# RWKV state kept block-diagonal, with neighbouring chunks of odd channel tiles in each other's place

## The chip, the core and the metric

The kernel runs on one core of a Trainium2 chip. The metric is device time in microseconds (us) of one execution, as the median of several runs. Engines are named as the profile names them: PE is TensorE's matmul (PEld its weight load), DVE is VectorE, ACT is ScalarE, POOL is GpSimd and SP is SyncE, which here only issues DMAs. L788 is line 788 of the kernel before.

## What is computed

One decoder layer over 1024 tokens and 1024 channels: a norm, one wide projection, RWKV-7 time mixing beside an attention that selects 256 keys by an indexer, gates that merge the two, an output projection, and a SwiGLU feed-forward part between two norms. The change is in the time mixing. It has 8 heads of 64 channels, and each head carries a state of 64 by 64 from token to token:

```python
def step(state, inp):
    r_t, d_t, k_t, v_t, kk_t, a_t = inp
    sa = jnp.einsum('bhij,bhj->bhi', state, -kk_t)
    state = (state * d_t[:, :, None, :]
             + sa[..., None] * (kk_t * a_t)[:, :, None, :]
             + v_t[..., None] * k_t[:, :, None, :])
    y_t = jnp.einsum('bhij,bhj->bhi', state, r_t)
    return state, y_t

_, y = lax.scan(step, state0, (tm(r_h), tm(decay), tm(k_h), tm(v_h), tm(kk), tm(a_h)))
```

Then y is normalised per head, a bonus term is added, and the sum is multiplied by a gate.

## The kernel before, in words

**Layout.** Everything is kept transposed, with channels on partitions. A channel tile has 128 channels, so it holds two heads; the four tiles 0 to 3 of the time mixing hold the eight heads, and a tile with an odd number is called an odd tile here. The big matmuls take two fp32r parts of each operand, high and low (`mm3`, L135): columns of 512 tokens, three products for each of the eight contraction tiles.

**The order of PE** is the program's own, written by hand. The big matmuls are generators that stand in a list named `fill`; `pump(n)` (L163) takes some n matmuls from it, and the recurrence calls it between its dependent products. The other engines' orders are made by the scheduler from the order of the program.

**Projections.** `proj_rwkv` (L302) makes the fourteen tiles r, k, v (four each), the low-rank inputs of decay and a (one tile) and the gate (one tile). Each result is shifted by a token into a staging tile `stg` (two buffers) and stored to DRAM (`d_rw`) by one DMA of 512 KB on SP's queue (L307; for decay and a at L404).

**The time mixing** (`rwkv`, L517) goes through the 1024 tokens in four quarters of 256, and each quarter has four chunks of 64 tokens. Two neighbouring chunks are a pair. A quarter loads its tiles back (L528), makes tanh of the low-rank products (L551), sums the log decay by chunk (L558), takes exponentials (P, L562), copies the decay over a whole chunk to PC (L566), and builds for every chunk two tables on the token axis, read rows and key rows (`AR`, `BK`), the masked products between them (`MT`, L667), a transposed copy (`NAT`, L686), and the inverse of a triangular matrix for each head and chunk (`TT`, L698 to L759).

Which half of 128 rows a chunk uses goes by its parity `pa` in the pair: `ba = 64 - 64 * pa` are the rows of the solve, `kb = 64 * pa` those of keys and outputs. All heads of a step have the same `ba`.

**The recurrence** (L778 to L845) has one step for each chunk, sixteen in all:

1. *read*: `AR` times the state, 8 products (64 rows contracted, 128 results, 64 columns), even and odd heads into two PSUM tiles (L787 to L790);
2. DVE adds the `ba` half to `rhs` (L794), ACT copies the `kb` half to the output buffer `y2` (L795); then a pump of 6 or 8;
3. *solve*: `TT` times `rhs`, 8 products of 64 by 64 (L800), which ACT copies, negated, into `UV` (L802); then a pump, or the `finish` of the pair before;
4. *update*: `NAT` times `UV`, 8 products (128 rows contracted, 64 results, 64 columns) (L810); DVE adds the old state (L813) and multiplies by PC (L814), into one of two state buffers; then a pump of 7 or 9 after the first chunk of a pair.

After both chunks of a pair come the *output* `MT` times `UV` (L821), `inner` (L741: the next pair's `rhs`, 16 products of 64 by 64 at L745, for both chunks in turn), the norm of y (L828 to L839), and later `finish` (L762): a transpose back, scale and bias by ACT (L771), the bonus by DVE (L773), the gate (L774), and a store to DRAM that the merge of that half reads.

The state's tile is `[128, 4, 64]`: for tile ct, rows 0 to 63 hold the even head's state and rows 64 to 127 the odd head's.

Of the kernel before, what the change touches and what calls it, by code (L numbers as in the profile page):

```python
# [11 lines left out]
F32 = mybir.dt.float32  # L12
# [6 lines left out]
AF = mybir.ActivationFunctionType  # L19
ALU = mybir.AluOpType  # L20
# [3 lines left out]
S = 1024  # L24
# [25 lines left out]
def block_kernel(ctx: ExitStack, tc: tile.TileContext, ins: dict, outT: bass.AP, stop=None, dbg=None):  # L50
# [15 lines left out]
    kc = cp.tile([128, 2, 128], F32, name="kc")  # L66
    state = cp.tile([128, 4, 64], F32, tag="S", name="S", bufs=2)
    G.dma_start(kc, ins["consts"][:, 0:2, :])
# [221 lines left out]
    def shifted(st, half, ct, x):  # L290
# [8 lines left out]
        else:  # L299
            V.scalar_tensor_tensor(s[:, 0:1], halo[:, ct:ct + 1], mu, s[:, 0:1], op0=ALU.mult, op1=ALU.add)  # L300

    def proj_rwkv(us, pj, groups):  # L302
        for g0, n in groups:
            for j in range(n):
                st = stage(pj)
                yield from proj(g0 + j, us, lambda half, ps: shifted(st, half, g0 + j, ps))
                SY.dma_start(d_rw[g0][j], st.rearrange("p h t -> p (h t)"))  # L307

# [183 lines left out]
    V.memset(state, 0.0)  # L492
    sref = [state]

# [22 lines left out]
    def rwkv(half, p, consts, ready=None):  # L517
# [5 lines left out]
        for q in range(2 * half, 2 * half + 2):  # L523
# [17 lines left out]
            for c in range(2):  # L541
                pss = [mix(), mix()]
                for e in range(2):
                    ct = 2 * c + e
                    for i, ps in enumerate(pss):
                        half_ = slice(64 * i, 64 * i + 64)
                        T.matmul(ps[:, e * 256:(e + 1) * 256], wup[half_, ct * 128:(ct + 1) * 128], wa[half_, :],
                                 start=True, stop=True)
                for i, t in enumerate((L, ta)):
                    for ct in (2 * c, 2 * c + 1):  # L550
                        A.activation(t[:, ct, :], pss[i][:, ct % 2 * 256:ct % 2 * 256 + 256], AF.Tanh, scale=0.5,  # L551
                                     bias=hb[:, 4 * i + ct:4 * i + ct + 1])
            sg = gd
# [126 lines left out]
            NAT = []  # L680
# [81 lines left out]
            def finish(pr, yc, y2):  # L762
# [7 lines left out]
                for ct in range(4):  # L770
                    A.activation(yT[:, ct, :], pt[:, ct * 128:(ct + 1) * 128], AF.Identity,  # L771
                                 scale=par[:, P_LG + ct:P_LG + ct + 1], bias=par[:, P_LB + ct:P_LB + ct + 1])
                V.tensor_tensor(yT, yT, bon[:, :, pr * 128:(pr + 1) * 128], op=ALU.add)  # L773
                V.tensor_tensor(yT, yT, pg.rearrange("p (c t) -> p c t", c=4), op=ALU.mult)  # L774
# [4 lines left out]
            for pr in range(2):  # L779
                yb = p.tile([128, 2, 512], F32, tag=("P", "x6")[pr], name="yb")  # L780
                yc, y2 = yb[:, 0, :], yb[:, 1, :]
                for pa in range(2):
                    c = 2 * pr + pa
                    ba, kb = 64 - 64 * pa, 64 * pa
                    st = sref[0]
                    as_ = [mix(), mix()]
                    for h, ct, ro, hc in hd:  # L787
                        T.matmul(as_[h % 2][:, ct * 64:ct * 64 + 64],  # L788
                                 AR[ro, ct, c, :, :].rearrange("p s t -> p (s t)"), st[ro, ct, :],
                                 start=True, stop=True)  # L790
                    for g in range(2):
                        a4 = as_[g][:, 0:256].rearrange("p (c t) -> p c t", c=4)
                        r4 = rhs.rearrange("p (c g t) -> p c g t", c=4, g=2)[ba:ba + 64, :, g, :]
                        V.tensor_tensor(r4, a4[ba:ba + 64], r4, op=ALU.add)  # L794
                        A.activation(y2.rearrange("p (c g t) -> p c g t", c=4, g=2)[kb:kb + 64, :, g, :],  # L795
                                     a4[kb:kb + 64], AF.Copy)
                    pump(6 if half == 0 else 8)
                    ps = mix()
                    for h, ct, ro, hc in hd:
                        T.matmul(ps[ba:ba + 64, hc], TT[ba:ba + 64, pr, h, :], rhs[ba:ba + 64, hc],  # L800
                                 start=True, stop=True)
                    A.activation(UV[pr][ba:ba + 64, pa, :], ps[ba:ba + 64, :], AF.Copy, scale=-1.0)  # L802
                    if late and pa == 1:
# [5 lines left out]
                    for h, ct, ro, hc in hd:  # L809
                        T.matmul(ps[ro, ct * 64:ct * 64 + 64], NAT[pr][:, pa, hc], UV[pr][:, pa, hc],  # L810
                                 start=True, stop=True)
                    new = cp.tile([128, 4, 64], F32, tag="S", name="S", bufs=2)
                    V.tensor_tensor(new, ps[:, 0:256].rearrange("p (c t) -> p c t", c=4), st, op=ALU.add)  # L813
                    V.tensor_tensor(new, new, PC[:, :, c:c + 1].to_broadcast([128, 4, 64]), op=ALU.mult)  # L814
                    sref[0] = new
                    if pa == 0:
# [675 lines left out]
```

## Time and profile before

| What | Value |
|---|---|
| Median of 3 runs | 1748.55 us (1747.58 to 1753.21) |
| The profiled execution's own time | 1748.71 us |
| Its span in the profile | 1746.9 us |
| Busy: PE, DVE, ACT | 98%, 64%, 48% of the span |
| Recurrence, first product to last | 446.9 to about 951 us, in four stretches |
| Matmul records of the solve, read, update | 256 each (two for each f32 product) |
| Clock granted to TensorE | 0.996 of full speed |

The profile shows one execution. Its rows give an engine, a line, an operation, what it writes and reads (`out<-in`), a count, and times; a group's row has busy us, mean ns, and the idle time before it with what ended that. Matmuls are pipelined, so their durations overlap; the distance from one start to the next says what a block costs.

### The profile page before, as it was taken

The numbers are of one execution on the slowest core, as the hardware profiler recorded it, in microseconds if no ns is written. First come the engines' busy times: TensorE is split into PE (matmuls) and PEld (weight loads), VectorE is DVE, ScalarE is ACT, GpSimd is POOL, SyncE is SP. The second block draws the span as 40 slices with busy tenths as digits, with TensorE's granted clock in tenths as the row PEclk, the third lists the DMA queues.
The fourth block names the chain that finished last, engine by engine and source line by source line (L and its number), as shares of the span: only waits on it lengthen the run. The fifth ranks groups of instructions, "written<-read, shape, count | busy, mean of one in ns | idle before, by whom it ended". The sixth has DMA issues, their size and how long they took to land.

```text
span 1746.9 us, 26692 instructions
## 1 busy us (share of the span) xinstructions
PE 1708.1 (98%) x10156; PEld 1410.3 (81%) x10156; DVE 1114.3 (64%) x2133; ACT 833.3 (48%) x1547; POOL 100.5 (6%) x123
## 2 busy tenths in 40 slices
PE   8999999999999998999999999999999999999997
PEld 6888888778878776878787888888788888888887
DVE  6789899857468567857876655445465564454464
ACT  6365998453445687645333455433234322232241
POOL 0000000010021111000100321000000000000000
PEclk9999999999999999999999999999999999999999
DMA  5542224536357535644343765173464344434442
GB/s 210 173 138 94 97 97 145 163 97 171 100 178 201 149 121 157 197 146 118 97 127 93 234 165 138 61 225 113 165 213 140 109 136 151 136 96 150 139 124 93
DMA packets 132383, 247.14 MB, mean 141 GB/s; under 512 B 36848, under 2 KB 60080, under 8 KB 132128
## 3 DMA queue, kind: packets, MB, share of 16 engines
q1 hardware_dynamic: 108896, 171.61, 31.7%
q10 hardware_dynamic: 15552, 47.75, 8.7%
q0 software_dynamic: 7808, 26.09, 5.6%
q8 instruction: 80, 1.31, 0.3%
q14 instruction: 47, 0.39, 0.1%
HBM read 192.40 MB, written 53.00 MB: 140 GB/s over the span
## 4 chain that ended last, share of the span: by engine, by line
PE 50%; issue 1%; DVE 1%; ACT 0%; POOLq 0%; POOL 0%; DVEq 0%; ACTq 0%
PE acc L145 14%; PE acc L140 13%; PE acc L141 13%; PE acc L156 3%; PE mix L1053 1%; PE mix L1029 1%; PE mix L1043 1%; PE acc L1197 0%; PE mix L800 0%; PE mix L788 0%; PE acc L1201 0%; ACT whi L114 0%; DVE h L1272 0%; PE mix L254 0%; PE mix L810 0%
## 5 line engine op out<-in xcount | busy, mean ns | idle before, releaser
L115 DVE TENSOR_TENSOR wlo<-wst,whi 128x1024 fp32r<-128x1024 f32 (+1 forms) x229 | 277.5, 1214 | 276.0 <-PE acc L145 132.7
L114 ACT ACTIVATE whi<-wst 128x1024 fp32r<-128x1024 f32 (+1 forms) x229 | 238.3, 1043 | 262.7 <-PE acc L141 186.9
L140 PE MATMUL acc<-zhi,whi 128*128 128x512 f32 x672 | 264.8, 394 | 0.0
L141 PE MATMUL acc<-zlo,whi 128*128 128x512 f32 x672 | 262.0, 390 | 0.0
L145 PE MATMUL acc<-zhi,wlo 128*128 128x512 f32 x672 | 170.2, 392 | 0.0
L140 PEld LDWEIGHTS acc<-zhi,whi 128*128 128x128 f32 x672 | 126.2, 188 | 26.8 <-issue 1.9
L141 PEld LDWEIGHTS acc<-zlo,whi 128*128 128x128 f32 x672 | 126.3, 188 | 24.8
L145 PEld LDWEIGHTS acc<-zhi,wlo 128*128 128x128 f32 x672 | 124.8, 188 | 25.4 <-issue 0.7
L140 PE MATMUL acc<-u1hi,whi 128*128 128x512 f32 x352 | 140.5, 399 | 0.1
L141 PE MATMUL acc<-u1lo,whi 128*128 128x512 f32 x352 | 137.6, 391 | 0.0
L140 PE MATMUL acc<-u0hi,whi 128*128 128x512 f32 (+1 forms) x352 | 135.5, 387 | 1.7 <-DVE tmp L323 1.7
L141 PE MATMUL acc<-u0lo,whi 128*128 128x512 f32 (+1 forms) x352 | 133.8, 383 | 0.0
L140 PE MATMUL acc<-fhi,whi 128*128 128x512 f32 (+1 forms) x318 | 114.3, 368 | 2.3 <-ACT whi L114 1.5
L141 PE MATMUL acc<-flo,whi 128*128 128x512 f32 (+1 forms) x318 | 112.9, 364 | 0.2 <-DVE flo L115 0.2
L145 PE MATMUL acc<-u1hi,wlo 128*128 128x512 f32 x352 | 90.0, 394 | 0.0
L145 PE MATMUL acc<-u0hi,wlo 128*128 128x512 f32 (+1 forms) x352 | 85.7, 384 | 0.0
L114 ACT ACTIVATE fhi<-tmp 128x512 fp32r<-128x512 f32 x44 | 27.7, 630 | 112.6 <-DVE tmp L1229 112.3
L140 PEld LDWEIGHTS acc<-u0hi,whi 128*128 128x128 f32 x352 | 66.2, 188 | 14.9 <-ACT stg L114 2.1
L140 PEld LDWEIGHTS acc<-u1hi,whi 128*128 128x128 f32 x352 | 66.2, 188 | 14.8 <-issue 1.3
L141 PEld LDWEIGHTS acc<-u1lo,whi 128*128 128x128 f32 x352 | 66.2, 188 | 12.6
L141 PEld LDWEIGHTS acc<-u0lo,whi 128*128 128x128 f32 x352 | 66.2, 188 | 12.1
L145 PEld LDWEIGHTS acc<-u1hi,wlo 128*128 128x128 f32 x352 | 64.9, 188 | 13.7 <-issue 0.9
(328 smaller groups left out, 3204.2 us busy)
## 6 DMA issues: line engine op xcount, KB each, us to landing
wst<-in_w_ffn_in SPq DMA_DIRECT2D x72, 512.0 KB, 3.6
wst<-in_w_in ACTq DMA_DIRECT2D x36, 512.0 KB, 4.5
wst<-in_w_in SPq DMA_DIRECT2D x27, 512.0 KB, 4.0
wst<-in_w_fo SPq DMA_DIRECT2D x25, 512.0 KB, 3.8
k<-d_k POOLq DMA_DIRECT2D x24, 512.0 KB, 7.9
h<-in_xT SPq DMA_DIRECT2D x32, 256.0 KB, 5.2
d_g<-tmp ACTq DMA_DIRECT2D x32, 256.0 KB, 3.4
tmp<-d_g SPq DMA_DIRECT2D x32, 256.0 KB, 3.7
```

The source lines that it names most:

```text
L114: A.activation(hi, x, AF.Copy)
L115: V.tensor_tensor(lo, x, hi.bitcast(F32), op=ALU.subtract)
L140: T.matmul(ps, whi[:, wk + k, :], ahi[:, ak + k, tok], start=k == 0, stop=False)
L141: T.matmul(ps, whi[:, wk + k, :], alo[:, ak + k, tok], start=False, stop=False)
L145: T.matmul(ps, wlo[:, wk + k, :], ahi[:, ak + k, tok], start=False, stop=k == nk - 1)
L156: T.matmul(ps, w[:, k, :], a[:, k, tok], start=k == 0 and w is whi and a is ahi, stop=k == nk - 1 and a is alo)
L1029: T.matmul(ps[:, :w], q[bi // 2][:, e, bi % 2 * 128:bi % 2 * 128 + 128], k[:, i, e, c:c + w], start=i == 0, stop=i == 1)
L1043: T.transpose(ps[:, j * 128:(j + 1) * 128], L[:, (c + j) * 128:(c + j + 1) * 128], ident)
L1053: T.matmul(py[64 * e:64 * e + 64, bi * 128:(bi + 1) * 128], v[:, j, 64 * e:64 * e + 64], pts[e][j // 4][:, j % 4, :], start=j == b, stop=j ...
```

## The change

**Storage.** For odd tiles of r, k and v the two chunks of each pair are stored in each other's place. `proj_rwkv` does this at the store, with two DMAs whose runs are 64 elements long; even tiles are stored as before. The tanh for decay and a of odd tiles writes its two halves swapped (two ACT operations of 128 columns in place of one of 256), PC is copied so that it stays in true order, and `finish` swaps back (two ACT operations for an odd tile, and the bonus in three DVE adds in place of one).

**Step.** A step still handles one true chunk of all heads. For odd tiles that chunk lies in the other slot, so its `ba` and `kb` are the other halves: `at[0]` is for even tiles, `at[1]` for odd ones. The eight heads of the solve are issued in the order 0, 2, 1, 3, 4, 6, 5, 7.

**State.** The tile becomes `[128, 4, 2, 64]`, a 128 by 128 block for each channel tile with the two heads' states on its diagonal and zeros beside them, in one buffer. The read becomes four products (128 rows contracted, 128 results, 128 columns) into one PSUM tile. The decay is multiplied into the whole state after the read; after the update's product DVE multiplies the product by PC into a `tmp` buffer and adds it to the two diagonal blocks. The core of the diff:

```diff
-    state = cp.tile([128, 4, 64], F32, tag="S", name="S", bufs=2)
+    state = cp.tile([128, 4, 2, 64], F32, name="S")
...
+    def swapped(x):
+        return x.rearrange("p (n s t) -> p n s t", s=2, t=64)
...
-                SY.dma_start(d_rw[g0][j], st.rearrange("p h t -> p (h t)"))
+                if g0 in (CT_R, CT_K, CT_V) and j % 2:
+                    d, t = (swapped(x) for x in (d_rw[g0][j], st.rearrange("p h t -> p (h t)")))
+                    for i in range(2):
+                        SY.dma_start(d[:, :, i, :], t[:, :, 1 - i, :])
+                else:
+                    SY.dma_start(d_rw[g0][j], st.rearrange("p h t -> p (h t)"))
...
-                        A.activation(t[:, ct, :], pss[i][:, ct % 2 * 256:ct % 2 * 256 + 256], AF.Tanh, scale=0.5,
-                                     bias=hb[:, 4 * i + ct:4 * i + ct + 1])
+                        x, y = pss[i][:, ct % 2 * 256:ct % 2 * 256 + 256], t[:, ct, :]
+                        xy = [(x, y)] if ct % 2 == 0 else [(swapped(x)[:, :, j, :], swapped(y)[:, :, 1 - j, :])
+                                                           for j in range(2)]
+                        for x, y in xy:
+                            A.activation(y, x, AF.Tanh, scale=0.5, bias=hb[:, 4 * i + ct:4 * i + ct + 1])
...
-            V.tensor_copy(PC, P[:, :, :, 64])
+            V.tensor_copy(PC[:, 0::2, :], P[:, 0::2, :, 64])
+            for i in range(2):
+                V.tensor_copy(PC[:, 1::2, i::2], P[:, 1::2, 1 - i::2, 64])
...
-                    A.activation(yT[:, ct, :], pt[:, ct * 128:(ct + 1) * 128], AF.Identity,
-                                 scale=par[:, P_LG + ct:P_LG + ct + 1], bias=par[:, P_LB + ct:P_LB + ct + 1])
-                V.tensor_tensor(yT, yT, bon[:, :, pr * 128:(pr + 1) * 128], op=ALU.add)
+                    x, y = pt[:, ct * 128:(ct + 1) * 128], yT[:, ct, :]
+                    xy = [(x, y)] if ct % 2 == 0 else [(x[:, 64 - 64 * i:128 - 64 * i], y[:, 64 * i:64 * i + 64])
+                                                       for i in range(2)]
+                    for x, y in xy:
+                        A.activation(y, x, AF.Identity, scale=par[:, P_LG + ct:P_LG + ct + 1],
+                                     bias=par[:, P_LB + ct:P_LB + ct + 1])
+                b = bon[:, :, pr * 128:(pr + 1) * 128]
+                V.tensor_tensor(yT[:, 0::2, :], yT[:, 0::2, :], b[:, 0::2, :], op=ALU.add)
+                for i in range(2):
+                    y = yT[:, 1::2, 64 * i:64 * i + 64]
+                    V.tensor_tensor(y, y, b[:, 1::2, 64 - 64 * i:128 - 64 * i], op=ALU.add)
...
-                    ba, kb = 64 - 64 * pa, 64 * pa
-                    st = sref[0]
-                    as_ = [mix(), mix()]
-                    for h, ct, ro, hc in hd:
-                        T.matmul(as_[h % 2][:, ct * 64:ct * 64 + 64],
-                                 AR[ro, ct, c, :, :].rearrange("p s t -> p (s t)"), st[ro, ct, :],
-                                 start=True, stop=True)
+                    at = [(pa ^ x, 64 - 64 * (pa ^ x), 64 * (pa ^ x)) for x in range(2)]
+                    as_ = mix()
+                    for ct in range(4):
+                        T.matmul(as_[:, ct * 128:(ct + 1) * 128],
+                                 AR[:, ct, 2 * pr + at[ct % 2][0], :, :].rearrange("p s t -> p (s t)"),
+                                 state[:, ct, :, :].rearrange("p e t -> p (e t)"), start=True, stop=True)
...
+                    for x, (pp, ba, kb) in enumerate(at):
+                        r4 = tiles(x, rhs[ba:ba + 64, :])
+                        V.tensor_tensor(r4, tiles(x, as_[ba:ba + 64, :]), r4, op=ALU.add)
+                    for x, (pp, ba, kb) in enumerate(at):
+                        A.activation(tiles(x, y2[kb:kb + 64, :]), tiles(x, as_[kb:kb + 64, :]), AF.Copy)
+                    V.tensor_tensor(state.rearrange("p c e t -> p c (e t)"), state.rearrange("p c e t -> p c (e t)"),
+                                    PC[:, :, c:c + 1].to_broadcast([128, 4, 128]), op=ALU.mult)
...
-                    for h, ct, ro, hc in hd:
+                    for h, ct, ro, hc in (hd[i] for i in (0, 2, 1, 3, 4, 6, 5, 7)):
+                        ba = at[ct % 2][1]
                         T.matmul(ps[ba:ba + 64, hc], TT[ba:ba + 64, pr, h, :], rhs[ba:ba + 64, hc],
                                  start=True, stop=True)
-                    A.activation(UV[pr][ba:ba + 64, pa, :], ps[ba:ba + 64, :], AF.Copy, scale=-1.0)
+                    for x, (pp, ba, kb) in enumerate(at):
+                        A.activation(tiles(x, UV[pr][ba:ba + 64, pp, :]), tiles(x, ps[ba:ba + 64, :]), AF.Copy, scale=-1.0)
...
-                    new = cp.tile([128, 4, 64], F32, tag="S", name="S", bufs=2)
-                    V.tensor_tensor(new, ps[:, 0:256].rearrange("p (c t) -> p c t", c=4), st, op=ALU.add)
-                    V.tensor_tensor(new, new, PC[:, :, c:c + 1].to_broadcast([128, 4, 64]), op=ALU.mult)
-                    sref[0] = new
+                    new = tmp()[:, 0:256].rearrange("p (c t) -> p c t", c=4)
+                    V.tensor_tensor(new, ps[:, 0:256].rearrange("p (c t) -> p c t", c=4),
+                                    PC[:, :, c:c + 1].to_broadcast([128, 4, 64]), op=ALU.mult)
+                    for e in range(2):
+                        eo = slice(64 * e, 64 * e + 64)
+                        V.tensor_tensor(state[eo, :, e, :], state[eo, :, e, :], new[eo], op=ALU.add)
```

`tiles(x, y)` takes the even (x = 0) or odd (x = 1) channel tiles' 128 columns of y. The update's product reads `NAT` and `UV` at the slot `at[ct % 2][0]`.

More of the change, by code (lines that the diff above doesn't have):

```diff
@@ L492, in block_kernel @@
     V.memset(state, 0.0)
-    sref = [state]
     def rwkv_consts(p):
@@ new lines, in rwkv, with tiles @@
+                    as_ = mix()
[3 more added lines that the diff above has]
+                                 state[:, ct, :, :].rearrange("p e t -> p (e t)"), start=True, stop=True)
+                    def tiles(x, y):
+                        return y.rearrange("p (c t) -> p c t", c=4)[:, x::2, :]
+                    for x, (pp, ba, kb) in enumerate(at):
+                        r4 = tiles(x, rhs[ba:ba + 64, :])
+                        V.tensor_tensor(r4, tiles(x, as_[ba:ba + 64, :]), r4, op=ALU.add)
@@ L809, in rwkv @@
                     for h, ct, ro, hc in hd:
-                        T.matmul(ps[ro, ct * 64:ct * 64 + 64], NAT[pr][:, pa, hc], UV[pr][:, pa, hc],
+                        pp = at[ct % 2][0]
+                        T.matmul(ps[ro, ct * 64:ct * 64 + 64], NAT[pr][:, pp, hc], UV[pr][:, pp, hc],
                                  start=True, stop=True)
-                    new = cp.tile([128, 4, 64], F32, tag="S", name="S", bufs=2)
-                    V.tensor_tensor(new, ps[:, 0:256].rearrange("p (c t) -> p c t", c=4), st, op=ALU.add)
-                    V.tensor_tensor(new, new, PC[:, :, c:c + 1].to_broadcast([128, 4, 64]), op=ALU.mult)
-                    sref[0] = new
+                    new = tmp()[:, 0:256].rearrange("p (c t) -> p c t", c=4)
[4 more added lines that the diff above has]
+                        V.tensor_tensor(state[eo, :, e, :], state[eo, :, e, :], new[eo], op=ALU.add)
                     if pa == 0:
```

6 lines of the change are left out of this document (removed).

## The prediction

> **What bounds the kernel now.** I read the page first: the engines' busy shares, the slices, the chain that ended last.
>
> ```profile
> span 1746.9 us, 26692 instructions
> PE 1708.1 (98%) x10156; PEld 1410.3 (81%) x10156; DVE 1114.3 (64%) x2133; ACT 833.3 (48%) x1547; POOL 100.5 (6%) x123
> PE   8999999999999998999999999999999999999997
> PEclk9999999999999999999999999999999999999999
> PE 50%; issue 1%; DVE 1%; ACT 0%; POOLq 0%; POOL 0%; DVEq 0%; ACTq 0%
> ```
>
> TensorE (PE) is busy in nearly every slice at nearly the full clock, and the chain runs over PE; "issue" and VectorE (DVE) have 1% each. So time taken out of PE's instruction stream should shorten the span, unless PE then stands waiting. The change is made in the recurrence, so I read next the four stretches that hold its sixteen steps. A row has the stretch and its length, then the busy us (and instructions) of PE, PE's weight load, DVE, ACT and POOL, PE's clock, the DMA share and GB/s.
>
> ```profile
> 440.00:480.00 40.00, 39.73 (x543) 32.06 (x542) 17.91 (x34) 18.60 (x38) 1.64 (x1) 1.00 0.28 92
> 590.00:640.00 50.00, 49.34 (x638) 39.56 (x636) 29.08 (x65) 42.72 (x105) 5.71 (x6) 1.00 0.29 98
> 750.00:800.00 50.00, 49.32 (x583) 39.67 (x582) 28.02 (x51) 26.84 (x50) 2.79 (x2) 1.00 0.40 118
> 915.00:960.00 45.00, 44.54 (x471) 35.92 (x464) 26.30 (x44) 16.45 (x31) 1.64 (x1) 1.00 0.30 89
> ```
>
> In all four PE is full, while DVE works 45 to 58% of the time. The small dependent products of the recurrence are spaced by fill: matmuls of 512 columns that the pump lets in. A busy PE is not PE at its peak, so I price blocks by the distance between starts in the timeline of PE, where ends, which are modelled, don't enter.
>
> ```profile
> 449.48 0.39 PE L140 MATMUL acc<-u0hi,whi 128*128 128x512 f32 x1
> 449.71 0.39 PE L141 MATMUL acc<-u0lo,whi 128*128 128x512 f32 x1
> 450.03 1.14 PE L800 MATMUL mix<-rhs,TT 64*64 64x64 f32 x16
> 451.10 0.50 PE L140 MATMUL acc<-u0hi,whi 128*128 128x512 f32 x1
> ...
> 460.17 0.69 PE L810 MATMUL mix<-UV,NAT 128*64 128x64 f32 x16
> 460.69 1.10 PE L821 MATMUL mix<-UV,MT 128*64 128x64 f32 x32
> 461.72 1.15 PE L745 MATMUL mix<-UV,MT 64*64 64x64 f32 x32
> 462.80 1.11 PE L788 MATMUL mix<-S,AR 64*128 64x64 f32 x16
> 463.84 0.50 PE L140 MATMUL acc<-u0hi,whi 128*128 128x512 f32 x1
> 464.17 0.39 PE L141 MATMUL acc<-u0lo,whi 128*128 128x512 f32 x1
> ```
>
> Here each f32 product is two records (x16 for eight heads). A fill matmul takes 449.71 - 449.48 = 0.23 us. The solve (L800) takes 451.10 - 450.03 = 1.07 us, 67 ns a record; its eight products of 64 by 64 all sit in the same quarter of the array. The block L745 has products of the same size whose rows and columns change sides from one to the next: 462.80 - 461.72 = 1.08 us for 32 records, 34 ns each. The state's read (L788) takes 463.84 - 462.80 = 1.04 us; the first fill after it takes 464.17 - 463.84 = 0.33 us, and the last one before a small block 450.03 - 449.71 = 0.32 us: about 0.1 more than 0.23 on either side, where the tile shape changes.
>
> **The change part by part.** *The solve.* With the chunks swapped in odd tiles, L800's heads go in an order that alternates the two diagonal quarters. I price it like L745, at half of 1.08, 0.54 us. Per step 1.07 - 0.54 = 0.53 us goes; sixteen steps: **8.5 us**. The bounds: nothing (records still go one after another), and 8.5.
>
> [...]
>
> *The state's read.* Four products with all 128 rows and 128 columns take the place of eight with 64 rows and 64 columns. The same shape, f32, eight records, is found where the norm's factors are spread over columns.
>
> ```profile
> 50.83 0.84 PE L145 MATMUL acc<-u1hi,wlo 128*128 128x512 f32 x3
> 51.51 1.05 PE L254 MATMUL mix<-kc,rsk 128*128 128x128 f32 x8
> 52.32 0.48 PE L140 MATMUL acc<-u0hi,whi 128*128 128x512 f32 x1
> 52.63 0.39 PE L141 MATMUL acc<-u0lo,whi 128*128 128x512 f32 x1
> ```
>
> The block takes 52.32 - 51.51 = 0.81 us, the next fill 0.31, 0.08 more than 0.23; before it three fills take 0.68, so nothing is lost on entry. That makes 0.89 us, against 0.09 + 1.04 + 0.10 = 1.23 for the read of before. Per step 0.34, sixteen steps: **5.4 us**; the bounds are 0.15 a step (2.4 us, if the entries and exits stay) and 0.34.
>
> The update (L810) and the output (L821) keep their counts and shapes: no change on PE. Nothing is added to PE. What comes next is what the step adds on DVE and ScalarE (ACT). The rows are groups of instructions between 440 and 960 us.
>
> ```profile
> L794 DVE TENSOR_TENSOR rhs<-mix,rhs 64x256 f32<-64x256 f32 x32 | 12.2, 417 | 23.4 <-PE mix L788 14.3 <-ACT TT L759 8.9
> L800 PEld LDWEIGHTS mix<-rhs,TT 64*64 64x64 f32 x256 | 16.1, 135 | 5.7 <-issue 2.5 <-DVE rhs L794 1.4 <-ACT TT L759 0.4
> L771 ACT ACTIVATE yb<-mix,par 128x128 f32<-128x128 f32 x28 | 10.7, 456 | 5.6 <-PE mix L767 5.5
> L795 ACT ACTIVATE yb<-mix 64x256 f32<-64x256 f32 x32 | 10.7, 372 | 7.1 <-DVE rhs L794 7.0
> L802 ACT ACTIVATE UV<-mix 64x512 f32<-64x512 f32 x16 | 9.5, 593 | 11.6 <-PE mix L800 10.4 <-DVE wlo L115 1.2
> L551 ACT ACTIVATE x<-mix,hb 128x256 f32<-128x256 f32 x24 | 9.2, 487 | 0.5 <-PE mix L547 0.5
> L814 DVE TENSOR_TENSOR S<-S,PC 128x256 f32<-128x256 f32 x16 | 6.8, 424 | 0.5
> L828 DVE TENSOR_TENSOR yb<-mix,yb 128x512 f32<-128x512 f32 x8 | 5.5, 686 | 0.3 <-PE mix L821 0.2
> ```
>
> - *Decaying the state* is now a multiply of 128x512 ahead of the update, 0.69 us by L828. It lies beside the solve; behind it in DVE's queue stand the weights' low parts (L115) and the adds of the fill.
> - *After the update's product* come three dependent DVE operations (a multiply of 128x256, two adds of 64x256 at 0.42 by L794) where there were two. The timeline shows the tightest place:
>
> ```profile
> 601.39 0.69 PE L810 MATMUL mix<-UV,NAT 128*64 128x64 f32 x16
> ...
> 602.13 0.42 DVE L813 TENSOR_TENSOR S<-mix,S 128x256 f32<-128x256 f32 x1 [1.21 <-PE mix L810]
> ...
> 603.16 1.11 PE L788 MATMUL mix<-S,AR 64*128 64x64 f32 x16
> ```
>
> DVE begins 0.74 us after the product's start. Three operations of 0.42 (L813, L814 and L794 agree) with their gaps are some 1.3, and some 0.1 passes until PE starts: 2.2 us, where PE comes back after 1.77. This step waits 0.4. Where PE comes back 2.63 us later (460.17 to 462.80) the third operation is covered.
> - *Read to solve.* The two adds into rhs (L794) keep their size. But PE arrives earlier: with four fills between, after 0.81 + 0.08 + 4 x 0.23 + 0.09 = 1.90 us, while the adds end at 1.05 (the read's modelled end) + 0.1 + 0.84 = 1.99. In the eight steps of half 0, which have the smaller pump, I take 0.1 each: 0.8.
> - *ACT* copies the solve's result in two halves of 64x256, 2 x 0.37 against 0.59, and the two copies of L795 now share a bank with both adds (they waited 7.0 us for DVE before, too). The cover is the four to eight fills ahead of the update, 0.9 us or more; without it 0.15 x 16 = 2.4 us.
> - *DVE's queue.* A step adds 0.69 + 0.42 = 1.1 us of DVE, 17.8 us in all. With DVE half idle I take 1.0 us in all for PE standing behind it; the bounds are nothing and all of it.
>
> Waits on PE together: 0.4 + 0.8 + 1.0 = **2.2 us**; bounds 0 and, with DVE in line with PE, 17.8 + 0.4 = 18.2.
>
> *Preparation and finish.* Sixteen tanh (L551) become 32 of 128x128, at most 0.46 by L771: 16 x (0.92 - 0.49) = 6.9 us of ACT, 1.7 a quarter. They are hidden by the fill that the pumps let in before the norm's sums (16 to 30 units, 3.7 to 6.9 us) and the pumps behind it; without it, up to 6.9 us. PC takes three small copies instead of one. Each of the eight finishes gets two more ACT operations (at most 0.46 each) and two more DVE adds (at most 0.42 each); their result goes to DRAM for the merge, long after, and only the PSUM buffer and the staging tile come free up to 1 us later, beside a pump of 24 units or more. I count all this at nothing.
>
> *The stores.* Six of the fourteen projections go to DRAM as two DMAs each, in runs of 64 elements, on SP's queue.
>
> ```profile
> d_rw<-stg SPq DMA_DIRECT2D x14, 512.0 KB, 4.3
> d_w<-W SPq DMA_DIRECT2D x8, 128.0 KB, 5.7
> ```
>
> ```profile
> L307 SPq DMA_DIRECT2D d_rw<-stg x13: 319/320/1052, 72.3 to 250.7; - x13
> ```
>
> A whole store lands in 4.3 us. The inverse's store (d_w) has 1024 runs of 32 elements, as many as one half of a split store, and takes 5.7. So a split pair lands within 4.3 to 2 x 5.7 = 11.4 us. Thirteen stores from 72.3 to 250.7 are 14.9 us apart on average, and the staging tile is written again two stores later. Behind them on SP's queue stand weights for which three raw buffers wait. Cost: nothing; it begins when a pair takes over some 22 us.
>
> [...]
>
> **The sum.** The profiled execution took 1748.71 us (span 1746.9, 1.8 around it): 1748.7 - 8.5 - 5.4 + 2.2 = **1737.0 us**. It lies 0.16 above the median of 1748.55, so the forecast stands for both.
>
> **The rivals.**
> 1. *The quarters don't overlap.* The solve stays at 1.07 us; 1748.7 - 5.4 + 2.2 = 1745.5, too little to tell. For it: no row shows the two diagonal quarters, L745 is on the other two. Against it: L745's 34 ns. [...]
> 2. *DVE takes the freed time.* One mechanism: the longer step (1.1 us) goes in line with PE, in the stretches 440 to 960. It decides once a step waits more than the 0.87 us that it saves. At the bound of 18.2 us: 1748.7 - 13.9 + 18.2 = 1753.0, slower. For it: PE follows DVE closely at 603.16, and L795 and L802 queue behind each other. Against it: DVE idles 42 to 55% there, and L800 waited for L794 for only 1.4 us in all.
> 3. *Half is lost*: waits of 0.5 us a step, 8.0 in all: 1742.8, at the edge of what can be told.
>
> **How the numbers follow.** A measurement of this kernel can tell about 0.3%, 5.2 us, from no change. The forecast with the waits between 0 and about 5 us (1734.8 to 1740): 0.62. The first rival 0.08; the second 0.14; the third 0.11. The remaining 0.05 is a shift of the other queues' order that gives more than my sum. Faster by over 0.3% (under 1743.3): 0.62 + 0.05 and a third of the third rival's, 0.71. Within: the first rival and the rest of the third, 0.15. Slower: 0.14. The range goes from 1731, beneath the forecast without waits, up to 1750, which takes in the first and third rivals and the lower part of the second.
>
> **What would show it.** In the PE timeline after: the solve's start to the next at about 0.54 us, the read's at about 0.81 with no longer fill before it, sixteen times each. If the solve still takes 1.07, the first rival holds. DVE as releaser ahead of the read or the solve for more than some 5 us in all would show the second or third. The split stores should land in under 12 us, and no acc matmul should wait for a staging tile. My forecast is wrong if PE's waits in the four stretches grow by more than 8 us, or if the time goes in another stage.

## The result, and the profile after

The changed kernel takes **1758.35 us** (median of 17 runs, 1752.16 to 1762.28); the kernel before, run beside it, takes 1752.72 us (17 runs, 1747.39 to 1757.22). The ratio is **1.0034, 95% interval 1.0023 to 1.0045**: slower by a third of a per cent. Two executions among all the runs that follow, at 2831 and 7644 us, were disturbed and stand outside every ratio. The forecast was 1737.0 us, so the sign was wrong, and the time lies above the range of 1731 to 1750. The profiled execution of before, on whose 1748.71 us the sum was made, was one of its faster ones, 4.0 us under the median of the 17; the difference is therefore read from the ratio.

The page of after, its span, busy shares and chain:

```profile
span 1756.4 us, 26556 instructions
PE 1707.1 (97%) x10028; PEld 1408.7 (80%) x10028; DVE 1135.2 (65%) x2189; ACT 841.9 (48%) x1595; POOL 101.4 (6%) x123
PE 72%; DVE 12%; ACT 7%; issue 4%; DMA 4%; POOL 1%; SPq 0%; DVEq 0%; ACTq 0%; POOLq 0%
```

PE is busy for 1.0 us less than before, and the span is 9.5 us longer: PE stands. The chain's shares don't say where. VectorE (DVE) and ScalarE (ACT) have 12% and 7% here and had 1% and 0% before, but the chain of before adds up to 52% of its span, for it reaches back to 843 us only, behind three of the four stretches. In a second profile of each kernel, DVE has 5% in before and 6% in after, and ACT 3% in both. The four stretches of the recurrence (columns as in the prediction):

```profile
440.00:480.00 40.00, 38.30 (x512) 30.71 (x511) 21.68 (x42) 19.98 (x45) 1.64 (x1) 1.00 0.27 94
590.00:640.00 50.00, 47.44 (x587) 37.44 (x587) 32.77 (x75) 42.88 (x107) 5.97 (x7) 0.97 0.32 105
750.00:800.00 50.00, 45.27 (x514) 35.97 (x514) 28.90 (x49) 24.97 (x48) 1.95 (x1) 0.97 0.41 124
915.00:960.00 45.00, 43.36 (x533) 34.97 (x533) 25.97 (x46) 18.30 (x39) 1.64 (x1) 1.00 0.35 102
```

PE's busy time falls from 39.73, 49.34, 49.32 and 44.54 to these; DVE's rises by 3.8 and 3.7 us in the first two, by 0.9 in the third, and stays about level in the last. The windows are the same, the work in them is not quite: the four recurrences of after begin 0.5, 4.4, 5.8 and 11.6 us later. In two windows the granted clock, 1.00 before, is now 0.97: each holds a *slow stretch*, 3.4 us at a granted clock of 0.50. The one at 590 us lies ahead of its recurrence, which begins at 600.9 us.

Yet the blocks themselves became shorter, as the prediction wanted. The timeline of PE in after:

```profile
619.79 0.68 PE L828 MATMUL mix<-rhs,TT 64*64 64x64 f32 x16
620.40 0.50 PE L140 MATMUL acc<-u1hi,whi 128*128 128x512 f32 x1
...
794.18 0.39 PE L141 MATMUL acc<-mlo,whi 128*128 128x512 f32 x1
794.40 1.05 PE L810 MATMUL mix<-S,AR 128*128 128x128 f32 x8
795.21 0.48 PE L140 MATMUL acc<-mhi,whi 128*128 128x512 f32 x1
```

The solve (L828 now) takes 620.40 - 619.79 = 0.61 us instead of 1.07; the read (L810 now) takes 0.81 instead of 1.04, and the fill ahead of it 0.22 instead of 0.32. So the time is lost between the blocks. What PE's idle time in front of the read ended on, as us and times, in before and then in after:

```profile
  issue: 2.8, 7
...
  DVE S L814: 0.3, 1
```

```profile
  DVE S L847: 6.1, 7
  issue: 6.1, 4
```

L847 are the last adds of the update. The "issue" rows are weight loads alone; in after they stand at the same waits. Where the largest one comes from (step 9 to 10), before and then after, first on PE:

```profile
774.12 0.69 PE L810 MATMUL mix<-UV,NAT 128*64 128x64 f32 x16
...
776.75 0.66 PE L788 MATMUL mix<-S,AR 64*128 64x64 f32 x8
```

```profile
779.64 0.69 PE L840 MATMUL mix<-UV,NAT 128*64 128x64 f32 x16
...
784.68 0.69 PE L810 MATMUL mix<-S,AR 128*128 128x128 f32 x2 [2.35 <-DVE S L847]
```

From the update's start to the next read it was 2.63 us and is 5.04. DVE in before, and in after:

```profile
775.11 0.42 DVE L813 TENSOR_TENSOR S<-mix,S 128x256 f32<-128x256 f32 x1
775.56 0.42 DVE L814 TENSOR_TENSOR S<-S,PC 128x256 f32<-128x256 f32 x1
775.91 0.69 DVE L828 TENSOR_TENSOR yb<-mix,yb 128x512 f32<-128x512 f32 x1
...
782.65 0.69 DVE L839 TENSOR_TENSOR yb<-yb,yrs 128x512 f32<-128x512 f32 x1 [1.81 <-POOL yrs L838]
783.67 0.42 DVE L813 TENSOR_TENSOR S<-mix,S 128x256 f32<-128x256 f32 x1 [0.33 <-PE mix L810]
```

```profile
781.43 0.69 DVE L860 TENSOR_TENSOR yb<-mix,yb 128x512 f32<-128x512 f32 x1 [0.60 <-PE mix L853]
782.16 0.69 DVE L862 TENSOR_REDUCE mn<-yb 128x8 f32<-128x512 f32 x1
782.76 0.41 DVE L843 TENSOR_TENSOR tmp<-mix,PC 128x256 f32<-128x256 f32 x1
783.09 0.68 DVE L235 TENSOR_TENSOR sacc<-sacc,tmp 128x512 f32<-128x512 f32 x1
783.69 0.85 DVE L847 TENSOR_TENSOR S<-S,tmp 64x256 f32<-64x256 f32 x2
```

Before, DVE took up the state 0.99 us after the product's start and went on to the norm (L828) when it was done (the rows from 782.65 on are needed further down). After, the first two norm operations stand **ahead** of the state's product (L843), which starts 3.12 us after the update; then an add of the filling (L235) stands between the product and its adds. DVE even idles 0.60 us waiting for the *output's* product before all this. It is the order of DVE's queue, made when the kernel is built, not its load.

All sixteen steps, measured the same way: the start of a block's first matmul to the start of the next block's, as a difference from the profile of before, summed (the last column of three over the twelve places that have a next read).

| Kernel (below) | read to solve | solve to update | update to next read | sum |
|---|---|---|---|---|
| before, again | +0.03 | +0.10 | -0.01 | +0.1 |
| **after** | -1.26 | -4.94 | **+6.51** | **+0.3** |
| after, again | -1.25 | -4.83 | +6.51 | +0.4 |
| state alone | -2.14 | -0.45 | +5.99 | +3.4 |
| swap, solve in pairs | +0.33 | -2.34 | -0.09 | -2.1 |
| swap alone | +0.37 | -5.18 | +0.10 | -4.7 |
| after, own buffer | -1.42 | -4.11 | +3.04 | -2.5 |
| and priority | -0.78 | -6.14 | +3.97 | -3.0 |
| and late norm | -0.84 | -6.35 | +0.88 | -6.3 |
| swap and priority | +0.55 | -5.66 | +0.52 | -4.6 |

The rows of after, after again, own buffer, priority and late norm each have a slow stretch in one place of "read to solve", which adds some 1.5 us to that column. The steps were to give 11.7 us and give nothing.

### The profile page after: what moved, and what is told of

Its sections match the earlier page's. It is cut to its first block, busy times and chain, and to the rows that moved or that the text cites. A ratio compares the mean times of both kernels' runs of the same rounds, so it can differ in the third digit from the quotient of the medians.

```text
span 1756.4 us, 26556 instructions
## 1 busy us (share of the span) xinstructions
PE 1707.1 (97%) x10028; PEld 1408.7 (80%) x10028; DVE 1135.2 (65%) x2189; ACT 841.9 (48%) x1595; POOL 101.4 (6%) x123
## 4 chain that ended last, share of the span: by engine, by line
PE 72%; DVE 12%; ACT 7%; issue 4%; DMA 4%; POOL 1%; SPq 0%; DVEq 0%; ACTq 0%; POOLq 0%
PE acc L140 19%; PE acc L145 18%; PE acc L141 18%; PE acc L156 3%; ACT junkl L976 2%; PE mix L1085 2%; ACT junk L976 2%; PE mix L1061 2%; DVE wlo L115 2%; PE mix L1075 2%; PE mix L926 1%; DVE junk L973 1%; ACT whi L114 1%; PE acc L1229 1%; DMA TT<-d_w 1%
```

## The experiments

Theory A: the chain on DVE behind the update is late because of the queue's order; the product waits for a buffer that it shares with the filling (`tmp`), and other work is put ahead. Rival B: the chain is merely one operation longer. Rival C: the loss lies in the preparation of the swapped tiles. "Before" in each comparison is the kernel before, run on the same chip: 1750.20 us beside swap alone, own buffer, priority and the control; 1750.14 beside state alone, swap in pairs, stores and late norm; 1751.50 beside the repeats and the last version.

### Which half of the change: the state alone, the swap alone

*State alone.* The old chunks' places, with the block-diagonal state:

```diff
-    state = cp.tile([128, 4, 64], F32, tag="S", name="S", bufs=2)
+    state = cp.tile([128, 4, 2, 64], F32, name="S")
...
+                    for ct in range(4):
+                        T.matmul(as_[:, ct * 128:(ct + 1) * 128], AR[:, ct, c, :, :].rearrange("p s t -> p (s t)"),
+                                 state[:, ct, :, :].rearrange("p e t -> p (e t)"), start=True, stop=True)
+                    V.tensor_tensor(rhs[ba:ba + 64, :], as_[ba:ba + 64, :], rhs[ba:ba + 64, :], op=ALU.add)
```

> Only the block-diagonal state, without the swap: four 128x128 reads, one 64x512 add into rhs, the decay, the product and two adds; solve, finish, tanh and stores as before. Theory A (the chain on VectorE behind the update is late, because it is one operation longer, its product waits for a buffer shared with the filling and other work is put ahead of it): the read gains 0.15 to 0.25 us a step (2.4 to 4 us in all), the stretch from update to next read grows by about 6 us, so it is slower than before by 1 to 4 us (ratio 1.0005 to 1.0025). Rival B (the chain is only one operation longer, the order of the queue doesn't matter): growth of at most 3 us, 0 to 2 us faster than before. Rival C (the loss of after lies in the preparation of the swapped tiles): nothing is lost here, 2.4 to 4 us faster (ratio 0.9977 to 0.9986).

Measured: 1756.82 us, ratio **1.0035, 1.0022 to 1.0048**: as much as the whole change loses. The stretch from update to next read grows by 5.99 us, in the same steps and by nearly the same amounts as in after (2 to 3: +0.90, there +0.98; 8 to 9: +1.12, +1.00; 9 to 10: +2.38, +2.41). DVE at step 9 to 10:

```profile
783.69 0.69 DVE L825 TENSOR_TENSOR yb<-mix,yb 128x512 f32<-128x512 f32 x1 [0.69 <-PE mix L818]
...
785.02 0.41 DVE L808 TENSOR_TENSOR tmp<-mix,PC 128x256 f32<-128x256 f32 x1
...
785.95 0.84 DVE L812 TENSOR_TENSOR S<-S,tmp 64x256 f32<-64x256 f32 x2
```

The same order, without any swap: for the stretch that grew, C is out, and with B's bound of 3 us so is B as the whole cause. The time, 6 us over before, is 2 us more than A allowed; the steps account for 3.4 of it.

*Swap, solve in pairs; swap alone.* Both keep the old state, read and update, and have the whole preparation of the swap; the second has the alternating solve, the first this:

```diff
-                    for h, ct, ro, hc in (hd[i] for i in (0, 2, 1, 3, 4, 6, 5, 7)):
+                    for h, ct, ro, hc in (hd[i] for i in (0, 1, 4, 5, 2, 3, 6, 7)):
```

> The swap with all its preparation (split stores, split tanh, three copies for PC, split scaling and adds in finish, four adds into rhs, two copies for UV), with the old state, read and update, and the solve issued so that both heads of a tile and both tiles of one place follow each other, in place of alternating at each head. Theory A: the preparation is hidden; the solve stays between 0.6 and 1.07 us, so the time is that of before or up to 5 us under it (ratio 0.997 to 1.000). Rival C: the preparation costs about 5 us whatever the solve does, so 1 to 5 us slower than before (ratio 1.0005 to 1.003), with the growth outside the sixteen steps.

> The swapped chunks with the alternating solve, but the state, its read and its update as before (the adds into rhs are four of 64x128 in a step, where after has two of 64x256). PE saves 16 x 0.46 = 7.4 us at the solve. Theory A (the lengthened state chain and its buffer cost what was to be gained): ratio 0.996 to 0.999. Rival C (the swap's own preparation, stores and finish cost it): ratio 1.001 or more.

> The swap with the alternating solve and the old state, read and update, one more profile of it (no rank given to any operation). Solve to update shorter by 0.46 us in nearly all steps (6 to 7.5 us in all), update to next read within 1 us of before's over all steps; what the time of this kernel does not show of these 7 us is lost in the preparation: 2 us in place of 1.2 in front of the transposes of nq in the second preparation, and 1 to 2 us more at the masks of the fourth.

Measured: in pairs 1751.40 us, ratio 1.0007 (0.9996 to 1.0018), the solve at 0.89 us; alternating 1747.46 us, ratio **0.9988** (0.9978 to 0.9999). A profile of it (an execution of 1748.79 us) has the solve at 0.61 us. Neither shows growth from update to next read (-0.09 and +0.10 us). So the swap's gain is real, though its interval ends close to 1, but the steps' 2.1 and 4.7 us come out as 1.2 us lost and 2.1 us won: some 3 us go elsewhere, and C is right in a small way; the ratio in pairs lies in C's range, the alternating one in A's. The waits of PE that the preparation adds, us in all, times and the longest, in before and then in after:

```profile
PE mix L593 <- DVE nq L589: 1.2, 1, 1.2
...
PE mix L667 <- DVE MT L671: 1.0, 2, 0.8
```

```profile
PE mix L607 <- DVE nq L603: 2.0, 1, 2.0
...
PE mix L681 <- DVE MT L685: 1.7, 2, 1.1
...
PE mix L681 <- ACT bs L664: 1.0, 1, 1.0
```

The first rows are the second quarter's. There ACT's tanh is twelve operations in 3.64 us for eight in 3.03, so the scan and the exponentials come later, and the PC copies are three in front of nq: PE waits 0.8 more. By the distances between starts, the third quarter has 0.37 more at the same place, the fourth 0.34 more at the transposes of the norm's factors and 1.5 more at its masks (the other rows), where one wait of 0.9 goes. That is 0.8 + 0.4 + 0.3 + 1.5 - 0.9 = 2.1 us. PE's waits at nq and at the masks are the same in the profiles of the swap kernels, and those with before's preparation don't have them.

*Stores.* Before, with the odd tiles stored in two DMAs of 64-element runs, in their old places:

```diff
+                if g0 in (CT_R, CT_K, CT_V) and j % 2:
+                    d, t = (x.rearrange("p (n s t) -> p n s t", s=2, t=64)
+                            for x in (d_rw[g0][j], st.rearrange("p h t -> p (h t)")))
+                    for i in range(2):
+                        SY.dma_start(d[:, :, i, :], t[:, :, i, :])
```

> Before, with the stores of the odd tiles of r, k and v given as two DMAs of 64-element runs each, in their old places: the DMA side of the swap and nothing else. Theory A and rival B: within 1 us of before (ratio 0.9994 to 1.0006), since nothing waits for these stores in time. Rival C with the stores as its mechanism (shorter runs land later, and what loads the tiles again waits): slower by 2 to 5 us (ratio 1.001 to 1.003), with the growth between two recurrences.

Measured: 1750.17 us, ratio 0.9994 (0.9982 to 1.0006). The stores cost nothing. In after:

```profile
d_rw<-stg SPq DMA_DIRECT2D x12, 256.0 KB, 2.7
```

Half a store lands in 2.7 us; two in line are 5.4 by that, an estimate, within the 4.3 to 11.4 that the prediction gave a pair.

### Why the chain is late: buffer, order, norm

Three steps, each on top of the one before.

*Own buffer:* `BK1` names a buffer of the preparation, which nothing else uses during the recurrence.

```diff
-                    new = tmp()[:, 0:256].rearrange("p (c t) -> p c t", c=4)
+                    new = p.tile([128, 4, 64], F32, tag="BK1", name="new")
```

> After, but the product of the update goes to a buffer of its own and no longer to one of the four tmp buffers that the fill uses too. Theory A (the recurrence's DVE chain is late because its product waits for a shared buffer and other work is put ahead of it): PE's waits for the state at the read, 9 us in all after, fall below 4, the wait of 2.35 us ahead of the third read of the third quarter and the slow fill behind it go, and the ratio to before falls from 1.0034 to 0.998 to 1.001. Rival B (the chain is simply one operation longer, whatever buffer): waits and ratio stay, 1.002 to 1.005. Rival C (the loss lies in the preparation between the recurrences): the ratio stays above 1.002 though the waits go.

*And priority:* the adds into rhs, the copies into UV and the three state operations under `with tc.high_priority():`.

> As the one before, and the adds into rhs, the two copies of the solve's result and the three operations on the state are given to the scheduler ahead of the fill's work. Theory A: waits at the read, the solve and the update together fall below 5 us (some 17 after); ratio 0.994 to 0.998. Rival B: the longer chain stays, waits above 10 us, ratio above 1.000. Rival C: waits fall, ratio 0.998 to 1.002, with the loss still seen between the recurrences.

*And late norm:* the norm's last multiplication (yb by yrs, which GpSimd makes) is pinned behind the next state adds; for a quarter's last pair, half-way through the pump behind it.

```diff
-                V.tensor_tensor(yh, yh, rs.unsqueeze(2).to_broadcast([128, 8, 64]), op=ALU.mult)
+                norm = yh, rs
...
+                    if late and pa == 0:
+                        scaled(*norm)
```

> After, with an own buffer for the product, the step's operations ahead of others on VectorE and ScalarE, and the norm's last multiplication, which waits for GpSimd's power, held back behind the next state adds. Theory A: the waits of steps 2 to 3 and 10 to 11 go (1.0 and 1.5 us in the kernel without this edit), so 2 to 3 us under that kernel and 3 to 5 us under before (ratio 0.997 to 0.9985), the stretches from update to next read together at most 2 us over before's. Rival B: the stretches stay at 4 us over before's, and the time within 1 us of that kernel (ratio 0.9985 to 0.9995).

Measured: 1753.92 us, **1.0014** (1.0000 to 1.0027); 1748.69, **0.9988** (0.9975 to 1.0001); 1748.33, **0.9982** (0.9969 to 0.9995). From update to next read, over before: 6.51 in after, then 3.04, 3.97 and 0.88 us. Own buffer's ratio lies between the ranges of A and B, and priority's in that of C, above A's; only late norm's is where A put it. The steps are clearer than the times. With its own buffer the product at step 9 to 10 goes first, and that place and the one before, which had lost 2.41 and 1.00 us, lose nothing; the other places keep their loss. DVE there:

```profile
782.85 0.42 DVE L843 TENSOR_TENSOR new<-mix,PC 128x256 f32<-128x256 f32 x1
783.30 0.85 DVE L847 TENSOR_TENSOR S<-S,new 64x256 f32<-64x256 f32 x2
784.19 0.69 DVE L860 TENSOR_TENSOR yb<-mix,yb 128x512 f32<-128x512 f32 x1
```

With priority another wait comes up, at step 10 to 11 (+1.49 us there). DVE stands on the norm's multiplication while the state's product behind it could go:

```profile
784.22 0.69 DVE L875 TENSOR_TENSOR yb<-yb,yrs 128x512 f32<-128x512 f32 x1 [1.81 <-POOL yrs L874]
784.83 0.42 DVE L847 TENSOR_TENSOR new<-mix,PC 128x256 f32<-128x256 f32 x1
```

Before had this wait too, but there it ended sooner: the multiplication began at 782.65, and DVE then stood 0.33 us for the state's product (the row at 783.67 above). Here the product's matmuls had started at 782.12, 2.71 us before DVE took up their result. With the multiplication pinned behind:

```profile
786.95 0.43 DVE L851 TENSOR_TENSOR new<-mix,PC 128x256 f32<-128x256 f32 x1 [0.46 <-PE mix L847]
787.41 0.85 DVE L855 TENSOR_TENSOR S<-S,new 64x256 f32<-64x256 f32 x2
...
789.44 0.68 DVE L802 TENSOR_TENSOR yb<-yb,yrs 128x512 f32<-128x512 f32 x1
```

The place falls from +1.49 to -0.08. What stays is the longer chain where little covers it: step 4 to 5 keeps its +0.62 in after and in all three of these, which is B's part. In time, the priority's step down is clear from the intervals only against after; between the last two kernels the times don't tell, the steps do.

*The control:* the same priority in before.

> Before, with the same operations of its step ahead of the fill's work. Before has little waiting in its steps (about 3 us), so all theories expect 0.998 to 1.001; if it gains more than 0.3%, a gain of the kernel with priorities is not the change's.

Measured: 1752.03 us, ratio 1.0009 (0.9998 to 1.0020). The steps are as in before, but for one slow stretch of 1.4 us at step 8. Priority alone gives nothing there; by the steps, nothing in before was late.

### What repeats, and what belongs to one execution

> After, unchanged, measured a second time beside the others. If the waits in the profile of after belong to the kernel and not to one execution: a ratio of 1.0025 to 1.0045 again, with growth of 0.4 to 2.5 us from update to next read in the same steps (2 to 3, 4 to 5, 6 to 7, 8 to 9, 9 to 10) and 2 us in front of the transposes of nq in the second preparation. What belongs to one execution (the slow stretch behind the wait of step 10, differences in the first 45 us and around 585 us) may come out otherwise.

> Before, unchanged, one more profile: the steps of the recurrences agree with the first profile within 0.2 us each; the stretches between them may be longer by up to 4 us together, as in the profiles of the kernels that leave the preparation as it was, and then this much of the difference between the profiles of before and after is not the change's.

After again: 1755.91 us, ratio 1.0023 (1.0010 to 1.0035), just under the range expected; its steps repeat to within 0.1 us, and so does the 0.8 at nq. The slow stretch at step 10, which I had put down to one execution, came again. What did not is at the end of the second preparation: PE stood 2.95 us there in the first profile, with the slow stretch at 590 us behind it, and 0.67 us in the second. Before again: 1752.47 us, steps within 0.1 us, the rest of the span 3.7 us longer. So of the 9.5 us between the first two profiles some 4 are not the change's.

### A version that beats both

The runs point to keeping the swap and dropping the block-diagonal state: swap alone, with the adds into rhs, the UV copies and the state's two operations under priority.

> The swap with the alternating solve, the old state, read and update, and the step's operations ahead of others on VectorE and ScalarE. By the runs so far (the block-diagonal state alone costs 6 us, all of it between update and next read in the same steps as in after; the swap with the solve in pairs shows no such growth): the solve gains 0.46 us in each step, 7 us in all, nothing is lost behind the update, and the preparation takes back 1 to 3 us: 4 to 6 us faster than before (ratio 0.9966 to 0.9977). If the loss in after came from the alternating order itself (the two places end together, and so their copies collide on ScalarE), the stretch from update to next read grows here too and the time is that of before (ratio 0.9995 to 1.0005).

Measured: **1742.28 us** (6 runs, 1740.33 to 1746.73), ratio **0.9951, 0.9935 to 0.9967**, the fastest of all. That is more than was expected. DVE ended idle time of PE before its reads once, 0.5 us.

The steps explain 4.6 us of the 9; by that account alone it should equal the swap without priority. The rest lies outside the recurrences, where its profile is 3.7 us shorter than the first of before. The third preparation, from the last update to the next read, takes 129.8 us in it, 134.1 and 135.7 in the two profiles of before and 133.4 in the swap alone. PE's wait for the norm's factors there is not in its trace:

```profile
PE mix L612 <- ACT nrT L606: 1.7, 1, 1.7
```

```profile
PE mix L627 <- ACT nrT L621: 1.4, 1, 1.4
```

The first row is of before, the second of the swap alone. The two kernels with the whole change and priority lack that wait too, and their third preparations take 130.0 and 130.6 us. The fourth takes 125.5 us against 128.6 in the swap alone, with the same waits at the masks but no slow stretch behind them. The granted clock as a whole does not explain it: the profiled execution, the fastest of the six, has 0.997 against 0.994 in the swap alone, but the mean over all runs is 0.9953 against 0.9946, which over 1740 us is 1 us. What the priority changed on ACT there, and how much of the gain it is, was not tested by a run of its own.

## Why the prediction was wrong, point by point

- **The solve**: right, mis-sized a little. 0.61 us in place of 0.54, 38 ns a record: 0.46 x 16 = 7.4 us, not 8.5. The first rival (the quarters don't overlap) is out, and with it the bound of no saving: the two diagonal quarters, writing one PSUM tile, end in 0.61 us where one took 1.07. The two write different halves of the tile's partitions; what two that write the same ones would do was not tried.
- **The read**: right in kind. Where nothing waits, read to solve shrinks by 0.14 to 0.27 us and the entry by 0.08 to 0.09: 0.22 to 0.36 a step against 0.34.
- **Waits on PE, 2.2 us: the step that failed**, and in it the sentence on DVE's queue ("With DVE half idle I take 1.0 us in all for PE standing behind it") and the one before ("Where PE comes back 2.63 us later the third operation is covered"). The chain's own price was about right: at step 4 to 5, priced at 2.2 us in place of 1.77, the distance is 2.39 (+0.62). But that holds when the chain is next in the queue. At step 9 to 10, one of the places with 2.63, it came 3.12 us late with DVE hardly busier than before (28.90 against 28.02 us in that stretch). Twelve places were to lose under 2 us and lost 6.51. The prediction priced the product's operation and never asked who else holds the `tmp` buffer that it writes: the filling does (L235 reads it). Giving the product its own buffer took back 3.5 us of the 6.5, all of it between steps 8 and 10; the priority with the norm's multiplication held back took most of what was left.
- **The UV copies on ACT**, counted as covered by four to eight fills, were not in the second quarter. ACT in after, at step 4:

```profile
603.89 1.15 ACT L976 ACTIVATE junkl<-kept,z 128x1024 int8<-128x1024 f32 x1
...
605.16 0.78 ACT L831 ACTIVATE UV<-mix 64x256 f32<-64x256 f32 x2
```

  A 1.15 us operation of the attention stands ahead of them, and solve to update gains 0.05 us there, and at steps 5 to 7 loses 0.18, gains 0.45 and 0.03, where 0.46 was to be had. At step 1 the solve stands inside, 1.02 us from start to next, for the second add into rhs. Over all steps 4.94 of 7.4 us are left.
- **The second rival** ("DVE takes the freed time", 1753.0 us, 0.14) named the right engine but the wrong mechanism, load: five places of twelve lost 0.6 to 2.4 us and the others little. That its time is the nearest to what came (1.0034 x 1748.7 is 1754.6 us) is luck.
- **Preparation and finish at nothing**: 2.1 us, from the tanh and the PC copies in front of nq and from the masks. The tanh were cheaper than priced (0.6 us of ACT a quarter, not 1.7). The cover named was fill; at nq PE already waited 1.2 us for this very chain, so no cover was left there.
- **The stores**: right, nothing.

The sum by measurement: steps +0.3, preparation +2.1. One more wait stands in no term: ahead of the last matmul before the fourth recurrence PE is idle for 0.8 us in after and 0.6 the second time, up to 1.4 in the others with both halves of the change, and not at all with one half or none. Its row says "issue", so its cause is open. The difference measured was 5.6 and, the second time, 4.4 us. The rest, 1 to 2.5 us, fits slow stretches of TensorE. The mean granted clock is 0.9927 over the 12 runs of after again and 0.9948 over the 17 of before beside them; 0.0021 of 1756 us is 3.7 us of full-speed time, part of it under waits, and one stretch, 1.4 us at step 10, is in the steps' sum already. A slow stretch behind the waits at the fourth quarter's masks is in seven profiles with the swap (after twice, the swap in pairs and alone, own buffer, priority, late norm) and not in swap and priority; in after it is 3.41 us at a granted clock of 0.50, from 863.28 us. Of the five without the swap two have it, those of the control and of the split stores, whose times are that of before. So this part is argued, not shown.

## What to carry to other kernels

The dependent chain was not covered by the idle time of a half-idle engine, only by its place in the queue: at step 9 to 10 its first operation began 3.12 us after the update's start (0.99 before), on a DVE that was busy for 28.90 of 50 us. Look in the timeline for what may be put ahead of each operation of a lengthened chain, and who else holds the buffer that it writes. The faster solve, 7.4 us of PE, was worth what the chain behind it left over: the steps of after gained nothing, those of the swap with the old state, the shorter chain, 4.7 us, and this one beat both kernels. When a change has two halves, run each alone first: here one gained, the other lost three times as much.

## What the hardware showed that I had not expected

After the wait of 2.35 us in front of step 10's read, TensorE did not come back at full pace. PE in after:

```profile
784.68 1.97 PE L810 MATMUL mix<-S,AR 128*128 128x128 f32 x8 [2.35 <-DVE S L847]
786.30 0.77 PE L140 MATMUL acc<-mhi,whi 128*128 128x512 f32 x1
786.88 0.63 PE L141 MATMUL acc<-mlo,whi 128*128 128x512 f32 x1
787.30 0.63 PE L140 MATMUL acc<-mhi,whi 128*128 128x512 f32 x1
...
788.16 0.41 PE L140 MATMUL acc<-mhi,whi 128*128 128x512 f32 x1
788.41 0.40 PE L141 MATMUL acc<-mlo,whi 128*128 128x512 f32 x1
```

Fill matmuls stand 0.42 us apart instead of 0.23, the read takes 1.62 us instead of 0.81 to 0.91, and at 788.16, 3.5 us after the restart, the pace is back: 2.35 us of waiting, and then 1.4 more in read to solve. The granted clock (the number ahead of the DMA share) says the same:

```profile
784.77:788.18 3.41, 3.41 (x13) 3.02 (x14) 2.05 (x4) 0.63 (x1) 0.00 (x0) 0.50 0.30 105
```

In the clock records of before and after, every slow stretch ahead of the last 20 us is 3.41 us long, two in before and five in after. In windows of 5 us from 340 to 795 us, what the clock of nine other profiles lost fits stretches of that length or of twice it (0.90, 0.50 and 0.92 from 685 to 700 us in after again). The wait ahead of this one was 2.35 us, and it came twice at the same place: in after again PE was idle for 2.35 us between 775 and 785 us, and the mean granted clock of the second half of that stretch is 0.66. That the wait brought it on is likely, not shown: the control has the same loss of 1.4 us at step 8, where nothing in the 3.4 us before the clock fell made PE wait longer than 0.26 us.

```profile
759.61:763.02 3.41, 2.89 (x82) 2.52 (x82) 0.66 (x2) 3.24 (x9) 0.00 (x0) 1.00 0.90 297
763.02:766.44 3.42, 3.42 (x10) 2.20 (x10) 0.68 (x2) 1.94 (x4) 0.00 (x0) 0.50 0.03 6
```
